# Another place modulo 256 bytes for fourteen w1 products behind each Strassen chunk, and a Strassen chunk directly behind w2

## The chip, the core and the metric

The kernel runs on one core of one Trainium2 chip. The metric is the device time of one execution in microseconds (us), from runs on the chip; before the change it is 2177.1 us, the median of three runs (2176.02 to 2177.48). TensorE (PE in the rows) multiplies, VectorE (DVE) and ScalarE (ACT) prepare operands, SyncE (SP) issues the DMAs.

## What is computed

Two transformer layers over 256 tokens of width 2048: stick-breaking attention and an MLP, then native sparse attention and an MLP, all in float32. The change touches the two MLPs alone.

```python
D_MODEL, SEQ, D_FF = 2048, 256, 4 * 2048

def sqrelu_mlp(h, w1, w2):
    return jnp.square(jax.nn.relu(h @ w1)) @ w2

for layer in range(DEPTH):          # DEPTH = 2
    h = h + attention[layer](rms_norm(h, g_attention[layer]))
    h = h + sqrelu_mlp(rms_norm(h, mlp_norm_g[layer]), mlp_w1[layer], mlp_w2[layer])
```

## The kernel before

Every float32 product is made of three products in a faster 32-bit format: an operand is split into a high part (`hi`, made by ScalarE) and the rest (`lo`, made by VectorE as operand minus `hi`), and `hi*hi + hi*lo + lo*hi` is summed in PSUM. Weights come in **chunks** of 512 KB: `load` issues one DMA from SP's queue into one of five `raw` buffers, `split` makes `hi` and `lo` of it, in one of four buffers each. A buffer of the pool is free again when its last reader is done.

The hidden width of 8192 is done in four groups (`fg` 0 to 3) of 2048. In `mlp`, `group1` multiplies by 2048 columns of w1, in four blocks (`fb` 0 to 3) of 512 columns with eight chunks each; `group2` then multiplies the squared result by the matching 2048 rows of w2. There are three kinds of chunk:

- a **w1 chunk** (`chunk_T`, L186): the weights are the stationary operand (128x128), x is the moving one (256 columns). 24 products: for each of eight 128x128 tiles, `hi` with `xhi` and with `xlo` (16 products), then `lo` with `xhi` (8 products).
- a **w2 chunk** (`chunk_N`, L156): y is stationary, the weights are moving (512 columns); 12 products.
- a **Strassen chunk** (`chunk_S`, L253): a part of w2 (column blocks 2 and 3 of four) that is done with seven instead of eight block products, by sums of weights (`ts`, made by VectorE, then split) and sums of y (`ss`); 21 products with 256 moving columns. Its own split `shi`, `slo` has a single buffer. VectorE makes `ts` in three steps (L226, L232, L233), then `slo` (L234) and the `lo` of the sums (L136). After eight such chunks `add_S` reads their four PSUM banks (pool `att`, four buffers).

`group2` does column blocks 0 and 1 as 16 w2 chunks and lays the eight Strassen chunks of block 2 between them, the i-th after w2 chunk j with j >= 2 + 1.6 i. Block 3 of group `fg` is done as eight Strassen chunks beside w1 of group `fg + 1`: `step`, behind chunks 2 and 5 of each block of w1. Only the last group does block 3 within `group2`, and group 0's w1 has no Strassen chunks beside it. So there are six w1 stages with eight Strassen chunks each, three in each MLP.

`split` puts a tile's data at an offset within its buffer, in elements of four bytes: `NEAR` 0, `TURN` 8, `FAR` 16, `SUM` 48, `SUM0` 60. All these buffers, and x, y and `ss`, begin at 128 modulo 256 bytes, so that `FAR` begins at 192, `TURN` at 160, `SUM` at 64 and `SUM0` at 112 modulo 256. Before the change w1 chunks lie at `FAR`, except the first of a stage with Strassen chunks, which lies at `TURN`; Strassen chunks beside w2 have `shi` at `SUM0`, those beside w1 have it at `SUM`; w2 chunks lie at `NEAR`.

The order of the work on each engine follows the order of the code for TensorE; a scheduler places the VectorE and ScalarE instructions between, so their order is read from the built program.

Of the kernel before, what the change touches and what calls it, by code (L numbers as in the profile page):

```python
# [8 lines left out]
F32 = mybir.dt.float32  # L9
F32R = mybir.dt.float32r  # L10
AF = mybir.ActivationFunctionType
OP = mybir.AluOpType
# [3 lines left out]
P = 128  # L16
# [3 lines left out]
KD = D // P  # L20
NB = 512
# [4 lines left out]
KC = 2  # L26
# [13 lines left out]
def hybrid_kernel(  # L40
# [6 lines left out]
    nc = tc.nc  # L47
# [4 lines left out]
    whi = ctx.enter_context(tc.tile_pool(name="whi", bufs=4))  # L52
    wlo = ctx.enter_context(tc.tile_pool(name="wlo", bufs=4))
# [70 lines left out]

    PAD = 64
    NEAR, FAR, TURN, SUM, SUM0 = 0, 16, 8, 48, 60

# [9 lines left out]
    def load(src, k0, nk, n0, nn):  # L139
        raw = wraw.tile([P, nk, nn], F32, tag="raw", name="raw")  # L140
        nc.sync.dma_start(
            raw, src[k0 * P:(k0 + nk) * P, n0:n0 + nn].rearrange("(k p) n -> p k n", p=P)
        )
        return raw

    def load_split(*where, o=(NEAR, NEAR)):
        return split(load(*where), o)
# [27 lines left out]
                mm(ahi, lo[:, kk, :], k, t, False, last and kk == KC - 1)  # L175
            pump()

    def chunk_T(ps, src, k0, n0, first, last, nk=KC, o=None):

        nm = KC * NB // P // nk  # L180
        hi, lo = src if isinstance(src, tuple) else load_split(src, k0, nk, n0, nm * P, o=o or (FAR, FAR))
        tiles = [(kk, m) for kk in range(nk) for m in range(nm)]

        def mm(w, x, kk, m, s, e):
            o = ps[m // 2][:, (m % 2) * T:(m % 2 + 1) * T]
            nc.tensor.matmul(o, w[:, kk, m * P:(m + 1) * P], x[:, k0 + kk, :], start=s, stop=e, skip_group_check=True)  # L186

        for kk, m in tiles:
            mm(hi, xhi, kk, m, first and kk == 0 and m % 2 == 0, False)
            mm(hi, xlo, kk, m, False, False)  # L190
        pump()
        for kk, m in tiles:
            mm(lo, xhi, kk, m, False, last and kk == nk - 1)
        pump()

    def proj_T(ps, src, n0, nk=KC, turn=False, then={}):

        for i in range(KD // nk):
            k0 = i * nk
            o = TURN if turn and i == 0 else FAR  # L200
            chunk_T(ps, src, k0, n0, k0 == 0, k0 + nk == KD, nk, (o, o))
            if i in then:
                then[i]()

# [192 lines left out]
    def mlp(l, layer, junk, done, last=None):  # L397
        w1, w2 = mlp_w1[l], mlp_w2[l]
        ss = junk.tile([P, 2, KD // 2, 4, P], F32R, name="ss", bufs=1)
        row = junk.tile([P, T], F32, name="row", bufs=1)  # L400

        def rows():
            yield
            pb = bcast_rows(make_rstd(layer))
            nc.scalar.activation(row, pb[:, :T], AF.Copy)

        def in_S(fg, nb, o):

            for i in range(NK):
                if i == 0:  # L410
                    bs, s = banks_S(att, "att")
                chunk_S(s, w2, fg * KD + i * KC, nb * NB, i == 0, i == NK - 1, yhi, ylo, ss[:, 0], ss[:, 1],
                        koff=fg * KD, o=o)
                if i == NK - 1:
                    add_S(nb, bs, s, junk)
                yield

        def group1(fg, beside_w1):

            step = lambda: next(beside_w1)  # L420
            for fb in range(D // NB):
                ps = [bank(acc, "acc") for _ in range(NB // P // 2)]
                proj_T(ps, w1, fg * D + fb * NB, turn=fg > 0 and fb == 0,
                       then={2: step, 5: step} if beside_w1 else {})
                k, n = fb * (NB // P), NB // P
                a = junk.tile([P, n, T], F32, tag="pre", name="pre", bufs=1)
                for j in range(0, n, 2):
                    nc.vector.scalar_tensor_tensor(
                        a[:, j:j + 2, :], ps[j // 2].rearrange("p (m t) -> p m t", m=2), 0.0,
                        row.unsqueeze(1).to_broadcast([P, 2, T]), op0=OP.max, op1=OP.mult,  # L430
                    )
                s = junk.tile([P, n, T], F32, tag="sq", name="sq", bufs=1)
                nc.scalar.activation(s, a, AF.Square)
                nc.scalar.activation(yhi[:, k:k + n, :], s, AF.Copy)
                nc.vector.tensor_tensor(ylo[:, k:k + n, :], s, yhi[:, k:k + n, :].bitcast(F32), op=OP.subtract)

                sv = s.rearrange("p (j kk) t -> p j kk t", kk=2)
                a1, a2 = [[sv[:, :, kk, t * P:(t + 1) * P] for kk in (1, 0)] for t in range(NT)]
                q = junk.tile([P, 2, 4, P], F32, tag="sums", name="sums", bufs=1)
                nc.vector.scalar_tensor_tensor(q[:, :, 0, :], a2[0], -1.0, a2[1], op0=OP.mult, op1=OP.subtract)  # L440
                nc.vector.tensor_tensor(q[:, :, 2, :], a1[0], a2[0], op=OP.subtract)
                nc.vector.tensor_tensor(q[:, :, 1, :], a2[1], q[:, :, 2, :], op=OP.subtract)
                nc.vector.tensor_tensor(q[:, :, 3, :], a1[1], q[:, :, 1, :], op=OP.subtract)
                split_evac(ss[:, 0, k // 2:k // 2 + 2], ss[:, 1, k // 2:k // 2 + 2], q)

        def group2(fg, end):

            blocks = (0, 1, 3) if end else (0, 1)
            side, si = in_S(fg, 2, SUM0), 0
            for j in range(len(blocks) * NK):  # L450
                nb, i = blocks[j // NK], j % NK
                if i == 0:
                    ps = [bank(acc, "acc") for _ in range(NT)]
                out = last is not None and end and nb == 3
                chunk_N(ps, w2, fg * KD + i * KC, nb * NB, i == 0, i == NK - (2 if out else 1), yhi, ylo,
                        koff=fg * KD, by_token=out and i == NK - 1)
                if i == NK - 1:
                    if out:
                        add_out(nb, ps, last)
                        return  # L460
                    add_h(nb, ps)
                    if end and nb == 3:
                        done(nb, (att, "att"))
                if si < NK and j >= (3 + 1.75 * si if end else 2 + 1.6 * si):
                    next(side)
                    si += 1
                    if si == NK and end:
                        for n in range(3):
                            done(n, (att, "att"))

        spawn(rows(), 1)
        NK = KD // KC
        for fg in range(DFF // D):
            group1(fg, in_S(fg - 1, 3, SUM) if fg else None)
            group2(fg, fg == DFF // D - 1)


# [595 lines left out]
```

## Time and profile before

| | |
|---|---|
| median of three runs | 2177.1 us |
| the profiled execution | 2184.2 us, of which 2180.6 us from its first to its last instruction |
| TensorE busy | 2168.8 us (99%) |
| VectorE, ScalarE busy | 1593.0 us, 1188.2 us |
| granted TensorE clock | 0.999 of full speed over the span |
| six w1 stages with Strassen chunks | 109.53 us each |

The table is to be read from the top down: TensorE has hardly any idle time, so a shorter kernel needs fewer or shorter products, and a longer one needs TensorE to wait. Matmuls are pipelined, so a row's length in the timeline (its second number) overlaps the next row; what a piece of work costs is the distance from its start to the start of the next.

### The profile page before, as it was taken

To read this page: it belongs to the slowest core of one execution; us is meant where nothing else is said; L and a number is where in the kernel's file an instruction comes from. 1 tells how busy PE (TensorE), PEld (TensorE's weight loads), DVE (VectorE), ACT (ScalarE), POOL (GpSimd) and SP (SyncE) were. 2 spreads that over 40 slices of the span, in tenths; PEclk is the share of its full clock that TensorE was granted. 3 is DMA by queue.
4 is the path that set the end of the run, shared out by engine and by line. 5 is a ranking of instruction groups with operands and counts; after the bars stand their busy time and mean duration, and the time that the engine had idled before them with its cause. 6 is when DMAs were issued, how large, how long until landed. Compare 5 with 4: busy or idle time off the path is not lost.

```text
span 2180.6 us, 37293 instructions
## 1 busy us (share of the span) xinstructions
PE 2168.8 (99%) x14914; PEld 2000.9 (92%) x14914; DVE 1593.0 (73%) x2190; ACT 1188.2 (54%) x1591; POOL 42.5 (2%) x75
## 2 busy tenths in 40 slices
PE   9999999999999999999999999999999999999999
PEld 9999988998998999999898888889989989999998
DVE  4655556668778878778777877755778788787786
ACT  5555565545555455555546666654554545554553
POOL 0000000000000000000000011000000000000000
PEclk9999999999999999999999999999999999999999
DMA  7655555665665665665667554456556556656664
GB/s 223 204 176 173 164 174 176 187 198 178 209 194 183 203 194 185 221 194 182 201 183 221 164 145 135 137 164 188 181 201 190 191 182 215 198 176 212 194 196 162
DMA packets 260790, 406.35 MB, mean 186 GB/s; under 512 B 13188, under 2 KB 91912, under 8 KB 260616
## 3 DMA queue, kind: packets, MB, share of 16 engines
q1 hardware_dynamic: 259800, 403.52, 59.3%
q8 instruction: 116, 1.90, 0.4%
q10 hardware_dynamic: 816, 0.46, 0.1%
q14 instruction: 58, 0.48, 0.1%
HBM read 401.83 MB, written 2.10 MB: 185 GB/s over the span
## 4 chain that ended last, share of the span: by engine, by line
PE 96%; DVE 2%; DMA 1%; ACT 0%; issue 0%; POOL 0%; DVEq 0%; ACTq 0%; SPq 0%; POOLq 0%
PE acc L186 43%; PE acc L156 35%; PE att L253 12%; PE att L156 1%; DMA raw<-in_mlp_w_dram 1%; DVE lo L136 1%; PE att L310 1%; PE att L905 1%; PE att L897 0%; PE att L898 0%; PE att L899 0%; PE att L592 0%; PE att L640 0%; PE att L851 0%; DVE slo L234 0%
## 5 line engine op out<-in xcount | busy, mean ns | idle before, releaser
L134 ACT ACTIVATE hi<-raw 128x1024 fp32r<-128x1024 f32 x639 | 672.8, 1057 | 503.4 <-PE acc L186 229.0
L136 DVE TENSOR_TENSOR lo<-raw,hi 128x1024 fp32r<-128x1024 f32 x639 | 776.4, 1221 | 224.5 <-ACT hi L134 206.2
L186 PE MATMUL acc<-xs,hi 128*128 128x256 f32 x5360 | 679.5, 280 | 1.9 <-ACT hi L134 1.9
L186 PEld LDWEIGHTS acc<-xs,hi 128*128 128x128 f32 x5360 | 647.8, 189 | 3.1 <-ACT hi L134 2.1
L186 PE MATMUL acc<-xs,lo 128*128 128x256 f32 x2680 | 366.5, 280 | 0.0
L186 PEld LDWEIGHTS acc<-xs,lo 128*128 128x128 f32 x2680 | 335.7, 189 | 0.0
L156 PE MATMUL acc<-hi,yhi 128*128 128x512 f32 x828 | 324.9, 393 | 0.0
L156 PE MATMUL acc<-hi,ylo 128*128 128x512 f32 x828 | 323.3, 391 | 0.0
L134 ACT ACTIVATE hi<-ts 128x1024 fp32r<-128x1024 f32 x112 | 118.4, 1057 | 195.0 <-DVE ts L233 121.8
L156 PE MATMUL acc<-lo,yhi 128*128 128x512 f32 x828 | 223.1, 391 | 0.0
L226 DVE TENSOR_TENSOR ts<-raw 128x512 f32<-128x512 f32 x112 | 77.4, 691 | 169.9 <-DMA raw<-in_mlp_w_dram 169.7
L156 PEld LDWEIGHTS acc<-lo,yhi 128*128 128x128 f32 x828 | 154.6, 188 | 31.9 <-issue 0.4
L156 PEld LDWEIGHTS acc<-hi,ylo 128*128 128x128 f32 x828 | 155.7, 188 | 29.5 <-DVE ylo L297 0.2
L156 PEld LDWEIGHTS acc<-hi,yhi 128*128 128x128 f32 x828 | 155.6, 188 | 29.6 <-ACT yhi L296 0.2
L156 PE MATMUL acc<-hi,xs 128*128 128x512 f32 x704 | 177.2, 392 | 0.0
L156 PEld LDWEIGHTS acc<-hi,xs 128*128 128x128 f32 x704 | 130.4, 188 | 26.5
L136 DVE TENSOR_TENSOR lo<-ts,hi 128x1024 fp32r<-128x1024 f32 x112 | 136.6, 1220 | 12.0 <-ACT hi L134 11.2
L231 ACT ACTIVATE shi<-raw 128x768 fp32r<-128x768 f32 x112 | 94.0, 839 | 65.0 <-DMA raw<-in_mlp_w_dram 38.3
L234 DVE TENSOR_TENSOR slo<-raw,shi 128x768 fp32r<-128x768 f32 x112 | 106.6, 952 | 0.0
L156 PE MATMUL acc<-lo,xs 128*128 128x512 f32 x352 | 97.5, 397 | 0.0
L253 PE MATMUL att<-hi,ss 128*128 128x256 f32 x672 | 94.8, 277 | 0.0
L253 PEld LDWEIGHTS att<-hi,ss 128*128 128x128 f32 x672 | 85.5, 188 | 0.0
(248 smaller groups left out, 2132.2 us busy)
## 6 DMA issues: line engine op xcount, KB each, us to landing
raw<-in_mlp_w_dram SPq DMA_DIRECT2D x512, 512.0 KB, 4.3
raw<-in_sb_w_qkv_dram SPq DMA_DIRECT2D x95, 512.0 KB, 3.8
raw<-in_nsa_w_in_dram SPq DMA_DIRECT2D x50, 512.0 KB, 3.8
raw<-in_sb_w_out_dram SPq DMA_DIRECT2D x32, 512.0 KB, 4.0
raw<-in_nsa_w_in_dram SPq DMA_DIRECT2D x64, 256.0 KB, 3.4
raw<-in_nsa_w_out_dram SPq DMA_DIRECT2D x32, 512.0 KB, 3.7
w1t<-in_nsa_cmp_w_dram SPq DMA_DIRECT2D x8, 512.0 KB, 4.8
h<-in_x_dram SPq DMA_DIRECT2D x8, 256.0 KB, 4.8
```

The lines of the kernel that those rows point to most:

```text
L134: nc.scalar.activation(hi, raw, AF.Copy)
L136: nc.vector.tensor_tensor(lo, raw, hi.bitcast(F32), op=OP.subtract)
L156: mm = lambda a, b, k, t, s, e: nc.tensor.matmul(ps[t], a[:, k, t * P:(t + 1) * P], b, start=s, stop=e)
L186: nc.tensor.matmul(o, w[:, kk, m * P:(m + 1) * P], x[:, k0 + kk, :], start=s, stop=e, skip_group_check=True)
L226: nc.vector.tensor_tensor(ts[:, :2, :], flat[:, W:3 * W].rearrange("p (a n) -> p a n", a=2), b12, op=OP.subtract)
L231: nc.scalar.activation(hi, flat[:, :3 * W], AF.Copy)
L234: nc.vector.tensor_tensor(lo, flat[:, :3 * W], hi.bitcast(F32), op=OP.subtract)
L253: nc.tensor.matmul(ps[i], a, w, start=s, stop=e, skip_group_check=True)
L310: nc.tensor.transpose(ps[:, j * T + t * P:j * T + (t + 1) * P], h[:, t, (kp + j) * P:(kp + j + 1) * P], ident)
L905: nc.tensor.transpose(ptp[:w, j * P:(j + 1) * P], src(j), ident)
```

## The change

It does three things in both MLPs.

1. `group1` does the first Strassen chunk before its first w1 chunk, thus directly behind the last w2 chunk of the group before, with `shi` at `SUM0`; the second comes behind chunk 4 of block 0, the others behind chunks 2 and 5 of blocks 1 to 3 as before.
2. The w1 chunk right behind a Strassen chunk that stands beside w1 (seven in a stage) is split by the new `split_turn`: `hi` lies at `TURN` for seven of its eight tiles (fourteen products) and at `FAR` for the eighth, `lo` at `FAR`. ScalarE and VectorE do the split in two pieces, of 896 and 128 elements, where it was one of 1024. The first w1 chunk of the stage stays wholly at `TURN`; it now has a Strassen chunk ahead of it.
3. In `group2` (all groups but the last) the Strassen chunks come at j >= 1.5 + 1.5 i, so behind w2 chunks 2, 3, 5, 6, 8, 9, 11, 12, where they were behind 2, 4, 6, 7, 9, 10, 12, 14.

```diff
+    def split_turn(raw):
+        flat = raw.rearrange("p k n -> p (k n)")
+        n, c = KC * NB, KC * NB - P
+        h, l = whi.tile([P, n + PAD], F32R, tag="hi", name="hi"), wlo.tile([P, n + PAD], F32R, tag="lo", name="lo")
+        for a, b, o in ((0, c, TURN), (c, n, FAR)):
+            nc.scalar.activation(h[:, o + a:o + b], flat[:, a:b], AF.Copy)
+            nc.vector.tensor_tensor(
+                l[:, FAR + a:FAR + b], flat[:, a:b], h[:, o + a:o + b].bitcast(F32), op=OP.subtract
+            )
+        cut = lambda t, o: [t[:, o(j) + j * P:o(j) + (j + 1) * P] for j in range(n // P)]
+        return cut(h, lambda j: TURN if (j + 1) * P <= c else FAR), cut(l, lambda j: FAR)
...
     def proj_T(ps, src, n0, nk=KC, turn=False, then={}):
         for i in range(KD // nk):
             k0 = i * nk
-            o = TURN if turn and i == 0 else FAR
-            chunk_T(ps, src, k0, n0, k0 == 0, k0 + nk == KD, nk, (o, o))
+            o = (TURN, TURN) if turn and i == 0 else None if i - 1 in then else (FAR, FAR)
+            chunk_T(ps, src, k0, n0, k0 == 0, k0 + nk == KD, nk, o)
...
-                        koff=fg * KD, o=o)
+                        koff=fg * KD, o=o if i == 0 else o1)
...
         def group1(fg, beside_w1):
             step = lambda: next(beside_w1)
+            if beside_w1:
+                step()
             for fb in range(D // NB):
                 proj_T(ps, w1, fg * D + fb * NB, turn=fg > 0 and fb == 0,
-                       then={2: step, 5: step} if beside_w1 else {})
+                       then={i: step for i in ((2, 5) if fb else (4,))} if beside_w1 else {})
...
-                if si < NK and j >= (3 + 1.75 * si if end else 2 + 1.6 * si):
+                if si < NK and j >= (3 + 1.75 * si if end else 1.5 + 1.5 * si):
...
-            group1(fg, in_S(fg - 1, 3, SUM) if fg else None)
+            group1(fg, in_S(fg - 1, 3, SUM0, SUM) if fg else None)
```

(`chunk_T` with `o` None takes the tiles from `split_turn`; its products are the same, in the same order. A w1 stage has the same 32 w1 chunks and eight Strassen chunks before and after.)

**Where TensorE goes from w2 to w1.** In the first stage with Strassen chunks TensorE went from the last w2 chunk (L156, its `hi` and `lo` parts) straight into the first w1 chunk (L186); two more w1 chunks and then a Strassen chunk followed.

```order
L156 MATMUL acc<-hi,yhi 128x512
L156 MATMUL acc<-hi,ylo 128x512
L156 MATMUL acc<-lo,yhi 128x512 x4
L186 MATMUL acc<-xs,hi 128x256 x16
L186 MATMUL acc<-xs,lo 128x256 x8
```

Now the same first w1 chunk (here L206) follows the end of a Strassen chunk (L273), which follows w2; four more w1 chunks come before the next Strassen chunk.

```order
L273 MATMUL att<-hi,yhi 128x256
L273 MATMUL att<-hi,ylo 128x256
L273 MATMUL att<-slo,yhi 128x256 x2
L273 MATMUL att<-slo,ss 128x256
L273 MATMUL att<-lo,ss 128x256 x3
L273 MATMUL att<-lo,yhi 128x256
L206 MATMUL acc<-xs,hi 128x256 x16
L206 MATMUL acc<-xs,lo 128x256 x8
```

What moved is one Strassen chunk, from behind the third w1 chunk to ahead of the first; the turned first chunk now follows products of Strassen's shape and place.

**VectorE between the `slo` of two neighbouring Strassen chunks in w2.** In the first MLP's first `group2`, before: from `slo_5305` (the Strassen chunk behind w2 chunk 9) to `slo_5358` (the one behind chunk 10, with only that w2 chunk between them). `ts_5426` belongs to the next Strassen chunk, the `lo` from a `raw` to w2 chunks.

```order
L234 TENSOR_TENSOR slo_5305<-raw_5300,shi_5304 128x768
L136 TENSOR_TENSOR lo_5339<-raw_5335,hi_5337 128x1024
L232 TENSOR_TENSOR ts_5355<-ts_5355,raw_5353 128x256
L233 TENSOR_TENSOR ts_5355<-raw_5353,ts_5355 128x256
L136 TENSOR_TENSOR lo_5365<-ts_5355,hi_5363 128x1024
L226 TENSOR_TENSOR ts_5426<-raw_5424 128x512
L136 TENSOR_TENSOR lo_5392<-raw_5388,hi_5390 128x1024
L232 TENSOR_TENSOR ts_5426<-ts_5426,raw_5424 128x256
L233 TENSOR_TENSOR ts_5426<-raw_5424,ts_5426 128x256
L234 TENSOR_TENSOR slo_5358<-raw_5353,shi_5357 128x768
```

After, in the same `group2`, the last two Strassen chunks (`slo_5411` behind w2 chunk 11, `slo_5464` behind chunk 12). `ts_5565` belongs to the Strassen chunk that now follows w2 directly; its `raw_5563` takes the `raw` buffer that `lo_5445` frees.

```order
L254 TENSOR_TENSOR slo_5411<-raw_5406,shi_5410 128x768
L137 TENSOR_TENSOR lo_5445<-raw_5441,hi_5443 128x1024
L137 TENSOR_TENSOR lo_5471<-ts_5461,hi_5469 128x1024
L246 TENSOR_TENSOR ts_5565<-raw_5563 128x512
L137 TENSOR_TENSOR lo_5507<-raw_5503,hi_5505 128x1024
L252 TENSOR_TENSOR ts_5565<-ts_5565,raw_5563 128x256
L254 TENSOR_TENSOR slo_5464<-raw_5459,shi_5463 128x768
```

There is less VectorE work between the two `slo` than in the pair of before, but one step in it waits for a DMA that could only be issued two instructions earlier; and there are now four such pairs in a `group2` (behind chunks 2 and 3, 5 and 6, 8 and 9, 11 and 12) where there were two (6 and 7, 9 and 10).

## Rows read from the trace of the kernel before

**Rows 1.** The page: busy time; chain of waits by engine and by line.

```profile
PE 2168.8 (99%) x14914; PEld 2000.9 (92%) x14914; DVE 1593.0 (73%) x2190; ACT 1188.2 (54%) x1591; POOL 42.5 (2%) x75
...
PE 96%; DVE 2%; DMA 1%; ACT 0%; issue 0%; POOL 0%; DVEq 0%; ACTq 0%; SPq 0%; POOLq 0%
PE acc L186 43%; PE acc L156 35%; PE att L253 12%; PE att L156 1%; DMA raw<-in_mlp_w_dram 1%; DVE lo L136 1%; PE att L310 1%; PE att L905 1%; PE att L897 0%; PE att L898 0%; PE att L899 0%; PE att L592 0%; PE att L640 0%; PE att L851 0%; DVE slo L234 0%
```

**Rows 2.** Windows, L186 alone: stretch, length, busy (count), clock, DMA share, GB/s.

```profile
415.69:486.41 70.72, 70.72 (x626) 70.68 (x624) 1.00 0.67 192
550.27:659.80 109.53, 91.54 (x768) 90.75 (x767) 1.00 0.63 197
722.77:832.30 109.53, 91.54 (x768) 90.75 (x767) 1.00 0.62 193
...
1982.24:2091.77 109.53, 91.54 (x768) 90.76 (x767) 1.00 0.62 196
```

**Rows 3.** Timeline, TensorE, one w1 stage: start, length, instructions merged, count.

```profile
722.77 2.06 PE L186 MATMUL acc<-xs,hi 128*128 128x256 f32 x16
724.66 1.11 PE L186 MATMUL acc<-xs,lo 128*128 128x256 f32 x8
725.61 1.98 PE L186 MATMUL acc<-xs,hi 128*128 128x256 f32 x16
...
728.33 1.98 PE L186 MATMUL acc<-xs,hi 128*128 128x256 f32 x16
...
731.05 0.28 PE L253 MATMUL att<-shi,yhi 128*128 128x256 f32 x1
...
733.52 2.05 PE L186 MATMUL acc<-xs,hi 128*128 128x256 f32 x16
...
736.35 2.05 PE L186 MATMUL acc<-xs,hi 128*128 128x256 f32 x16
...
739.18 2.05 PE L186 MATMUL acc<-xs,hi 128*128 128x256 f32 x16
...
742.01 0.29 PE L253 MATMUL att<-shi,yhi 128*128 128x256 f32 x1
...
744.41 2.04 PE L186 MATMUL acc<-xs,hi 128*128 128x256 f32 x16
...
832.30 0.40 PE L156 MATMUL acc<-hi,yhi 128*128 128x512 f32 x1
```

**Rows 4.** Timeline: a Strassen chunk within w2, and what follows it.

```profile
717.61 0.28 PE L253 MATMUL att<-shi,yhi 128*128 128x256 f32 x1
...
720.02 0.39 PE L156 MATMUL acc<-hi,yhi 128*128 128x512 f32 x1
```

**Rows 5.** Waits of TensorE, 500:1010, then 1575:2180: total us, times, longest.

```profile
PE att L253 <- DVE slo L234: 1.0, 2, 0.6
...
PE att L253 <- DVE slo L234: 1.8, 2, 1.1
```

**Rows 6.** Timeline, VectorE, then TensorE, at neighbouring Strassen chunks; idle before in brackets.

```profile
522.12 0.95 DVE L234 TENSOR_TENSOR slo<-raw,shi 128x768 fp32r<-128x768 f32 x1
...
526.19 1.23 DVE L136 TENSOR_TENSOR lo<-ts,hi 128x1024 fp32r<-128x1024 f32 x1 [1.19 <-ACT hi L134]
...
529.87 0.95 DVE L234 TENSOR_TENSOR slo<-raw,shi 128x768 fp32r<-128x768 f32 x1
...
530.87 0.50 PE L253 MATMUL att<-slo,yhi 128*128 128x256 f32 x2 [0.60 <-DVE slo L234]
```

**Rows 7.** The page: groups (count, busy, mean ns, idle before, releaser); DMA issues.

```profile
L136 DVE TENSOR_TENSOR lo<-raw,hi 128x1024 fp32r<-128x1024 f32 x639 | 776.4, 1221 | 224.5 <-ACT hi L134 206.2
...
L226 DVE TENSOR_TENSOR ts<-raw 128x512 f32<-128x512 f32 x112 | 77.4, 691 | 169.9 <-DMA raw<-in_mlp_w_dram 169.7
...
L234 DVE TENSOR_TENSOR slo<-raw,shi 128x768 fp32r<-128x768 f32 x112 | 106.6, 952 | 0.0
...
raw<-in_mlp_w_dram SPq DMA_DIRECT2D x512, 512.0 KB, 4.3
```

More of the change, by code (lines that the diff above doesn't have):

```diff
@@ L176, in chunk_N, with chunk_T @@
             pump()
-    def chunk_T(ps, src, k0, n0, first, last, nk=KC, o=None):
+    def split_turn(raw):
[9 more added lines that the diff above has]
+        return cut(h, lambda j: TURN if (j + 1) * P <= c else FAR), cut(l, lambda j: FAR)
+    def chunk_T(ps, src, k0, n0, first, last, nk=KC, o=(FAR, FAR)):
         nm = KC * NB // P // nk
-        hi, lo = src if isinstance(src, tuple) else load_split(src, k0, nk, n0, nm * P, o=o or (FAR, FAR))
         tiles = [(kk, m) for kk in range(nk) for m in range(nm)]
+        if o is None:
+            hi, lo = split_turn(load(src, k0, nk, n0, nm * P))
+        else:
+            hi, lo = [
+                [w[:, kk, m * P:(m + 1) * P] for kk, m in tiles]
+                for w in (src if isinstance(src, tuple) else load_split(src, k0, nk, n0, nm * P, o=o))
+            ]
         def mm(w, x, kk, m, s, e):
             o = ps[m // 2][:, (m % 2) * T:(m % 2 + 1) * T]
[L186 to L190, printed above, removed]
+            nc.tensor.matmul(o, w, x[:, k0 + kk, :], start=s, stop=e, skip_group_check=True)
+        for (kk, m), w in zip(tiles, hi):
+            mm(w, xhi, kk, m, first and kk == 0 and m % 2 == 0, False)
+            mm(w, xlo, kk, m, False, False)
         pump()
-        for kk, m in tiles:
-            mm(lo, xhi, kk, m, False, last and kk == nk - 1)
+        for (kk, m), w in zip(tiles, lo):
+            mm(w, xhi, kk, m, False, last and kk == nk - 1)
         pump()
@@ L405, in rows, with in_S @@
             nc.scalar.activation(row, pb[:, :T], AF.Copy)
-        def in_S(fg, nb, o):
+        def in_S(fg, nb, o, o1):
             for i in range(NK):
@@ L448, in group2 @@
             blocks = (0, 1, 3) if end else (0, 1)
-            side, si = in_S(fg, 2, SUM0), 0
+            side, si = in_S(fg, 2, SUM0, SUM0), 0
             for j in range(len(blocks) * NK):
```

## Prediction

> **What bounds the kernel now.** I read the page first: TensorE is busy 99% of the span, and the chain of waits runs over TensorE for 96% of it; w1 and the other products of its form (L186) have 43%, w2 (L156) 35%, Strassen (L253) 12% [rows 1]. So a gain has to come from TensorE's own pace, and a loss from a wait that it does not have now. VectorE is at 73% [rows 1].
>
> Then the windows of L186. In the first w1 stage, which has no Strassen chunks, 624 products take 70.72 us, which is 113.3 ns for each; the six stages with Strassen chunks take 109.53 us each (three of the six are shown, the others have the same length), at a granted clock of 1.00 like the first [rows 2]. Such a stage has 768 w1 products and 8 x 21 Strassen products; at 113.3 ns the 936 would take 106.1 us. So 3.4 us of each stage is a slower pace that no clock and no wait explains.
>
> The timeline shows where. The first chunk, turned, takes 2.84 us (722.77 to 725.61), the two behind it 2.72 us each (113.3 ns for a product). The Strassen chunk at 731.05 takes 2.47 us (118 ns), and from there a w1 chunk takes 2.83 us (733.52 to 736.35 to 739.18; 117.8 ns) [rows 3]. The instructions, shapes, offsets and clock of the chunk at 725.61 and the one at 736.35 are the same. So there are **two paces for the same product**, and TensorE stays in one until a product of another kind comes: a turned chunk led into the fast one, the Strassen chunk into the slow one. The next Strassen chunk, entered from the slow pace, takes 2.40 us (742.01 to 744.41) and yet slow w1 follows [rows 3]. The stage ends at 832.30 with w2.
>
> **The fourteen turned products.** They remove nothing; their effect is on the chunks behind them. If they lead into the fast pace, as the turned chunk at 722.77 did, a stage is (where nothing else stands, from [rows 3]):
> - the Strassen chunk directly behind w2, like the ones within w2: 717.61 to 720.02, 2.41 us [rows 4]
> - the turned first chunk: 2.84 us
> - 24 chunks at the fast pace: 24 x 2.72 = 65.28 us
> - 7 Strassen chunks entered from the fast pace: 7 x 2.47 = 17.29 us
> - 7 chunks with fourteen turned products. The turned `hi` part has 16 products in 1.89 us (722.77 to 724.66), 118.1 ns each: 14 x 118.1 + 10 x 113.3 = 2.79 us, and 2.84 if all 24 go at the turned pace. I take 2.79, since the first unturned product behind the turned chunk is already fast: 7 x 2.79 = 19.53 us.
>
> Together 107.35 us against 109.53, 2.18 us less; six stages: **13.1 us**. Bounds: if no turned chunk works, 24 x 2.72 becomes 4 x 2.72 + 20 x 2.83 (the first chunk, still wholly turned, serves four), one Strassen chunk takes 2.47 and six 2.40, and the seven chunks 2.83: 109.4, a gain of 0.7 us in all. If the wholly turned first chunk fails too, now that a Strassen chunk stands ahead of it, 2.41 + 2.84 + 24 x 2.83 + 7 x (2.40 + 2.83) = 109.8, a loss of 1.5 us. No row shows fourteen turned products, or a turned chunk behind a Strassen chunk: the six turned chunks in the trace all stand behind w2 and all have 24. That is the main doubt, since the exit from a turned chunk may depend on how many products it has.
>
> **The split in two pieces.** On VectorE 1024 elements take 1221 ns and 768 take 952 [rows 7]: 1.05 ns an element and some 145 ns fixed, so a second piece costs 145 ns; ScalarE, at 54% [rows 1], gets a second piece as well. 42 chunks have it, 6 us of VectorE in all, none of it on the path: the w1 stages show no wait of TensorE at all in the lists of waits, which hold only L253 for `slo` (L234) [rows 5], and those fall in w2. Without that cover it would cost at most 6 us. The faster w1 asks VectorE for the same work in 2% less time, and it is 73% busy.
>
> **The moved Strassen chunks in w2.** Now two Strassen chunks stand with one w2 chunk between them at four places of a `group2` instead of two. `slo` has one buffer, so the second `slo` cannot be made before the first is used. The trace shows what that costs: VectorE made the first `slo` at 522.12, waited 1.19 us for ScalarE on the way, came to the second at 529.87, and TensorE stood 0.60 us until 530.87 [rows 6]: 7.75 us between the two `slo` were too many. All such waits together are 2.8 us, the longest 1.1 [rows 5]. In the new order the worst pair is the last. Between its two `slo` stand `slo`, a `lo`, a `lo`, the first `ts` step, a `lo` and a short `ts` step, by the steps between starts about 0.9 + 1.1 + 1.1 + 0.6 + 1.1 + 0.5 = 5.3 us, which would be no stall. But the `ts` step needs a buffer that the first of those `lo` frees; a DMA takes 4.3 us to land, and VectorE already waits for DMAs at this step 170 us in 112 cases, 1.5 us each [rows 7]. With 1.1 us of other work in between the wait is up to 3.2 us, so 5.3 to 8.5 us between the `slo`. Where 7.75 gave 0.6 us, 8.5 gives 1.35, and 5.3 gives none. I take 0.7 at that pair in each of the six `group2` that change, 4.0 us, in place of the 2.8 now: **1.2 us lost**; from 2.8 gained (no pair waits) to what the last rival says.
>
> **The Strassen chunk behind w2** reads PSUM banks that `add_S` must have left. Three w2 chunks, about 8.2 us, lie between the end of the chunk before and it, and its first product on such a bank comes some 0.8 us later. From the `slo` of the chunk before, wanted 0.8 us before that chunk's end, to `add_S`'s last read of these banks VectorE has three `lo` (1.2 us each), one `slo` (0.95) and six short steps (0.3 to 0.7, as the ones above): about 7.5 us [rows 7] in 9.8. I cost it at nothing; if that cover were gone, the wait would be a microsecond or two in six places.
>
> **Sum.** 13.1 gained, 1.2 lost, 11.9 us less. The profiled execution took 2184.2 us, so I expect 2172.3 in its terms, 0.5%; the median of the runs lies 7.1 below it, and 2177.1 - 11.9 = **2165.2 us**.
>
> **A rule that speaks against it.** The two paces above show the same instructions at 113.3 and 117.8 ns [rows 2, 3]. The Trainium skill's page "SBUF — State Buffer", section "Who interferes with whom", gives TensorE two independent read ports, one for the moving operand and one for the weights, and lets only the port pair that VectorE shares with GpSimd cause contention. By that rule the place of an operand cannot set the pace, and the turning would be worth nothing. The rows show a difference that follows neither clock nor shape, so I hold the rule as incomplete here; the rival just below carries its chance.
>
> **Rivals.**
> 1. *The turning does nothing behind a Strassen chunk.* For it: nothing in the trace shows it there, and a Strassen chunk entered from either pace left the slow one behind it [rows 3]. Against it: a turned chunk led into the fast pace from w2 each of six times. Time: 2177.1 - 0.7 + 1.2 = 2177.6, and with the first chunk failing too 2177.1 + 1.5 + 1.2 = 2179.8. By the page's rule on the ports it would also be about that.
> 2. *It works every other time*: it fails behind a Strassen chunk entered fast (2.47 us) and works behind one entered slow (2.40 us). Then the chunks behind turns one, three, five and seven (5, 4, 4 and 1) stay slow and ten chunks of 24 are fast: 2.41 + 2.84 + 10 x 2.72 + 14 x 2.83 + 4 x (2.47 + 2.83) + 3 x (2.40 + 2.79) = 108.8; six times 0.7, less 1.2: 2174.1.
> 3. *Slower: VectorE comes too late for the second `slo`.* Place: the pairs behind w2 chunks 5 and 6, 8 and 9, 11 and 12, eighteen places. If each cost 1.3 us, somewhat over the longest now, that is 23.4 less the 2.8 there now: 2177.1 - 13.1 + 20.6 = 2184.6. It decides from 15.9 / 18 = 0.9 us at each. For it: VectorE's waits for DMAs; against: the 5.3 us of work, and that only four waits are listed for the twelve such pairs of now [rows 5].
>
> **How the numbers follow.** Forecast 0.60 (2162 to 2169); rival 1 0.24, of which 0.16 at 2177.6 and 0.08 at 2179.8; rival 2 0.07; rival 3 0.09. The lower end takes the forecast with no wait left in w2, 2177.1 - 13.1 - 2.8 = 2161.2. Up to 2178.5 lie the forecast, rival 2 and the larger part of rival 1, 0.83. A measurement can tell about 0.2% (4.4 us): faster has the forecast and a little of rival 2, 0.62; slower rival 3 and a little of rival 1, 0.10; the rest, 0.28, is the same.
>
> **What would show it.** In the new trace: w1 stages of about 107.4 us; w1 chunks of 2.72 us from the second chunk behind each Strassen chunk on (2.83: rival 1; by turns: rival 2); Strassen chunks beside w1 of 2.47; waits of TensorE for L234's successor of about 4 us in all (over 16: rival 3). The forecast is wrong above all if the fourteen products end where the pace falls back.

## The result, and the profile after

The changed kernel takes 2192.1 us (median of 8 runs, 2182.4 to 2194.5); the kernel before takes 2178.5 beside it (8 runs). The ratio is 1.0055, 95% interval 1.0039 to 1.0072: **slower by about 12 us** (13.5 by the medians), where 12 us less was forecast. Two executions of the runs below, at granted clocks of 0.85 and 0.76 over their whole span, are left out of every figure. The profiled execution took 2194.2 us, of which 2192.5 are its span.

On the page after (its lines on busy time and on the chain of waits by engine, and one of its groups: busy, mean ns, idle before, releaser) the chain that set the end leaves TensorE far more often than in [rows 1]:

```profile
PE 2160.9 (99%) x14914; PEld 1989.1 (91%) x14914; DVE 1590.7 (73%) x2232; ACT 1188.8 (54%) x1633; POOL 42.5 (2%) x75
...
PE 80%; DVE 10%; DMA 6%; issue 3%; ACT 1%; POOL 0%; DVEq 0%; ACTq 0%; SPq 0%; POOLq 0%
...
L246 DVE TENSOR_TENSOR ts<-raw 128x512 f32<-128x512 f32 x112 | 77.4, 691 | 198.7 <-DMA raw<-in_mlp_w_dram 198.4
```

TensorE is on 80% of the chain (96% before), DMAs on 6% (1%). VectorE is no busier, but stands 198 us for DMAs at the first `ts` step, 170 before [rows 7].

The w1 stages did what was forecast. Windows of w1's line (L206 now; length, busy, clock, DMA share, GB/s), then TensorE's timeline of one stage (start, length, merged count):

```profile
725.14:832.56 107.42, 88.80 (x768) 88.31 (x768) 1.00 0.60 192
903.34:1010.76 107.42, 88.81 (x768) 88.31 (x768) 1.00 0.62 197
```

```profile
727.56 2.05 PE L206 MATMUL acc<-xs,hi 128*128 128x256 f32 x16
...
730.40 2.00 PE L206 MATMUL acc<-xs,hi 128*128 128x256 f32 x16
...
741.30 0.28 PE L273 MATMUL att<-shi,yhi 128*128 128x256 f32 x1
...
743.78 2.04 PE L206 MATMUL acc<-xs,hi 128*128 128x256 f32 x16
```

All six are 107.42 us (109.53 in [rows 2], 107.35 forecast). The wholly turned chunk takes 2.84 (727.56 to 730.40), four fast ones 10.90, the Strassen chunk 2.48; behind each Strassen chunk the fast pace comes back. That is 12.7 us less.

w2 lost more than that. From the start of w2 to the next stage the six took 382.3 us in all before and 405.4 after, **23.1 us more**; the rest of the span is 1.5 longer. Two of the six w2 stand behind the first w1 of an MLP, which has no Strassen chunks; they lost 2.4 us together, and the four behind stages with Strassen chunks lost 20.7. Windows of TensorE over the third w2 of the first MLP, of the kernel before and of the changed one (length, busy, clock, DMA share, GB/s):

```profile
832.30:895.92 63.62, 63.26 (x362) 1.00 0.60 198
```

```profile
832.56:903.34 70.78, 65.15 (x363) 0.98 0.57 186
```

TensorE's waits over the whole trace (total us, times, longest), and the two longest in that w2 in its timeline, with the idle time in brackets:

```profile
PE att L273 <- DVE slo L254: 14.2, 17, 2.4
PE att L273 <- ACT shi L251: 7.7, 4, 3.2
```

```profile
849.26 0.57 PE L273 MATMUL att<-shi,yhi 128*128 128x256 f32 x1 [3.20 <-ACT shi L251]
...
853.38 0.40 PE L157 MATMUL acc<-hi,yhi 128*128 128x512 f32 x1
...
894.23 0.50 PE L273 MATMUL att<-slo,yhi 128*128 128x256 f32 x2 [2.43 <-DVE slo L254]
```

Before, the waits for `slo` were 2.7 us, and none for `shi` was listed. The four waits for `shi` come one in each of the four w2 behind stages with Strassen chunks, at its second Strassen chunk, and are its first wait. So the waits do not fall on the last pair alone, which I had priced.

**Where the loss is made.** I worked out a *lead* from the trace: how long the `lo` of the first w2 chunk was ready before its first product. VectorE's `lo` for the first chunk of the w2 just shown, and TensorE's first products with it:

```profile
831.81 1.22 DVE L137 TENSOR_TENSOR lo<-raw,hi 128x1024 fp32r<-128x1024 f32 x1
```

```profile
834.40 1.07 PE L157 MATMUL acc<-lo,yhi 128*128 128x512 f32 x4
```

831.81 + 1.22 = 833.03, so 1.4 us. At the same w2 of the kernel before, 827.68 + 1.22 to 834.14 is 5.2 us:

```profile
827.68 1.22 DVE L136 TENSOR_TENSOR lo<-raw,hi 128x1024 fp32r<-128x1024 f32 x1
```

```profile
834.14 1.07 PE L156 MATMUL acc<-lo,yhi 128*128 128x512 f32 x4
```

At the three other w2 behind a stage with Strassen chunks the lead was 3.2, 2.5 and 3.6 us (before 7.0, 4.0 and 6.8). TensorE did not wait in w1, but VectorE fell behind there, and w2 started with less in hand. The experiments ask why.

### The profile page after: what moved, and what is told of

Its sections match the earlier page's. It is cut to its first block, busy times and chain, and to the rows that moved or that the text cites. A ratio compares the mean times of both kernels' runs of the same rounds, so it can differ in the third digit from the quotient of the medians.

```text
span 2192.5 us, 37357 instructions
## 1 busy us (share of the span) xinstructions
PE 2160.9 (99%) x14914; PEld 1989.1 (91%) x14914; DVE 1590.7 (73%) x2232; ACT 1188.8 (54%) x1633; POOL 42.5 (2%) x75
## 4 chain that ended last, share of the span: by engine, by line
PE 80%; DVE 10%; DMA 6%; issue 3%; ACT 1%; POOL 0%; DVEq 0%; ACTq 0%; SPq 0%; POOLq 0%
PE acc L206 40%; PE acc L157 27%; PE att L273 7%; DMA raw<-in_mlp_w_dram 6%; DVE lo L137 4%; DVE slo L254 2%; PE att L157 1%; DVE ts L246 1%; PE att L330 1%; DVE ts L252 1%; PE att L927 1%; PE att L919 0%; ACT hi L135 0%; DVE ylo L457 0%; DVE pre L450 0%
## 5 line engine op out<-in xcount | busy, mean ns | idle before, releaser
L137 DVE TENSOR_TENSOR lo<-raw,hi 128x1024 fp32r<-128x1024 f32 x597 | 725.0, 1220 | 225.8 <-ACT hi L135 208.6
L135 ACT ACTIVATE hi<-raw 128x1024 fp32r<-128x1024 f32 x597 | 627.8, 1057 | 439.3 <-PE acc L157 176.6
L206 PE MATMUL acc<-xs,hi 128*128 128x256 f32 x5360 | 669.8, 278 | 1.9 <-ACT hi L135 1.9
L206 PEld LDWEIGHTS acc<-xs,hi 128*128 128x128 f32 x5360 | 638.9, 188 | 2.6 <-ACT hi L135 2.1
L206 PE MATMUL acc<-xs,lo 128*128 128x256 f32 x2680 | 360.5, 277 | 0.0
L206 PEld LDWEIGHTS acc<-xs,lo 128*128 128x128 f32 x2680 | 330.4, 188 | 0.0
L273 PE MATMUL att<-hi,ss 128*128 128x256 f32 x672 | 96.4, 280 | 0.0
L273 PEld LDWEIGHTS att<-hi,ss 128*128 128x128 f32 x672 | 87.0, 190 | 0.0
```

Of the source, the lines that this page charges most:

```text
L135: nc.scalar.activation(hi, raw, AF.Copy)
L137: nc.vector.tensor_tensor(lo, raw, hi.bitcast(F32), op=OP.subtract)
L206: nc.tensor.matmul(o, w, x[:, k0 + kk, :], start=s, stop=e, skip_group_check=True)
L273: nc.tensor.matmul(ps[i], a, w, start=s, stop=e, skip_group_check=True)
```

## The experiments

Diffs are against the changed kernel. One edit comes back often; **"no chunk behind w2"** stands for:

```diff
             if beside_w1:
-                step()
...
-                       then={i: step for i in ((2, 5) if fb else (4,))} if beside_w1 else {})
+                       then={i: step for i in (2, 5)} if beside_w1 else {})
...
-            group1(fg, in_S(fg - 1, 3, SUM0, SUM) if fg else None)
+            group1(fg, in_S(fg - 1, 3, SUM, SUM) if fg else None)
```

"Stages" and "w2" are the sums in us over the six w1 stages with Strassen chunks and over the six w2 that lead into them, worked out from each run's trace; "lead" is that at the w2 just shown (the third of the first MLP). Ratios are to the kernel before on the same chip. A trace is one execution, and executions of one kernel lie up to 18.5 us apart here (e1_turn), so a ratio need not follow its trace exactly: the trace of e5_turn_pace is 8 us slower than the median of its runs, those of e9_one_lo, e6_raw6 and e4_old_pace are their quickest, that of e14_after_at5 its slowest. Where trace and ratio differ, the ratio decides.

| run | stages | w2 | lead | ratio (95%) |
|---|---|---|---|---|
| before | 657.2 | 382.3 | 5.2 | 1 |
| after | 644.5 | 405.4 | 1.4 | 1.0055 (1.0039 to 1.0072) |
| e1_turn | 645.2 | 390.5 | 1.7 | 1.0017 (1.0001 to 1.0033) |
| e2_pace | 657.2 | 379.2 | 6.7 | 0.9993 (0.9984 to 1.0002) |
| e3_no_turn | 656.1 | 393.1 | 3.6 | 1.0070 (1.0057 to 1.0082) |
| e4_old_pace | 661.6 | 389.5 | 2.1 | 1.0115 (1.0097 to 1.0132) |
| e5_turn_pace | 645.2 | 388.9 | 3.5 | 0.9977 (0.9961 to 0.9993) |
| e6_raw6 | 644.5 | 396.2 | 4.1 | 1.0031 (1.0017 to 1.0046) |
| e7_hi16 | 650.3 | 380.8 | 6.3 | 0.9970 (0.9958 to 0.9981) |
| e8_pace_raw6 | 657.2 | 386.6 | 6.6 | 1.0047 (1.0031 to 1.0063) |
| e9_one_lo | 645.2 | 381.5 | 5.2 | 0.9969 (0.9958 to 0.9980) |
| e10_pieces | 657.2 | 378.7 | 7.1 | 0.9994 (0.9986 to 1.0003) |
| e11_after_one_lo | 644.5 | 402.5 | 2.0 | 1.0049 (1.0030 to 1.0067) |
| e12_all24 | 651.4 | 383.2 | 5.4 | 0.9972 (0.9962 to 0.9982) |
| e13_second_at5 | 655.5 | 382.5 | 6.7 | 1.0008 (0.9999 to 1.0017) |
| **e14_after_at5** | 644.5 | 388.7 | 5.5 | **0.9968 (0.9957 to 0.9980)** |
| e15_one_lo_at5 | 644.5 | 387.5 | 6.4 | 0.9977 (0.9967 to 0.9986) |

### One part at a time

e1_turn: no chunk behind w2, and the old places in w2.

```diff
-                if si < NK and j >= (3 + 1.75 * si if end else 1.5 + 1.5 * si):
+                if si < NK and j >= (3 + 1.75 * si if end else 2 + 1.6 * si):
```

> Only the fourteen turned products; the order of the Strassen chunks is the one of the kernel before in w1 and in w2. Three theories on the 23 us that w2 of the changed kernel lost. Order: four Strassen pairs instead of two in a group2 ask VectorE for `slo` too soon; then w2 here is as before (about 63.7 us a group2), the w1 stage 2.84 + 23 x 2.72 + 8 x 2.79 + 8 x 2.47 = 107.5 us instead of 109.5, and the time 12 us below the kernel before. Lead: the faster w1 brings TensorE to w2 with VectorE further behind; then w2 here is longer by 12 us or more and the time no better than before. Split: the extra pieces on VectorE and ScalarE delay what w2 needs; then as for lead.

e2_pace: no chunk behind w2, and no turned products.

```diff
-            o = (TURN, TURN) if turn and i == 0 else None if i - 1 in then else (FAR, FAR)
+            o = (TURN, TURN) if turn and i == 0 else (FAR, FAR)
```

> Only the closer places of the Strassen chunks in w2 (due at 1.5 + 1.5 x si instead of 2 + 1.6 x si); no turned products, no Strassen chunk behind w2. Order: w1 stage 109.5 us, the six group2 longer by 15 to 23 us in all, TensorE's waits for `slo` and `shi` of about 20 us, time 15 to 23 us above the kernel before. Lead or split: w2 within 5 us of before, time within 5 us.

e3_no_turn has this last diff alone, and e4_old_pace the diff of e1_turn alone.

> The changed kernel without the fourteen turned products; the order in w1 and w2 is the changed one. Order: w1 stage 109.4 us, w2 longer by the same 23 us in all, time 23 us above the kernel before. Lead or split: w2 within 5 us of before, since w1 is as slow as before and nothing is split in two; time within 5 us.

> The changed kernel with the places of the Strassen chunks in w2 as before (2 + 1.6 x si). The last Strassen chunk of w2 then stands one w2 chunk ahead of the one directly behind w2, which uses the same PSUM banks. Order: the twelve places within w2 as before (about 3 us of waits), but at the end of each of the six w2 a wait for `add_S` of 3 to 4 us, some 20 us in all, w1 stages without it 107.5: time 5 to 12 us above the kernel before. If `add_S` is early enough: 12 us below the kernel before, and the closer places were not needed.

My first theory, that the closer places ask VectorE for `slo` too soon, fell. With the closer places alone TensorE's waits for `slo` nearly vanish; in the whole trace of e2_pace they are

```profile
PE att L273 <- DVE slo L254: 0.6, 2, 0.4
```

so four pairs instead of two cost nothing; w2 is 3.1 us shorter than before. Instead each of the other two edits lengthens w2, although neither changes w2's own products: turned products by 9.7 us (e5_turn_pace, below, against e2_pace), the chunk behind w2 by 13.9 (e3_no_turn against e2_pace), both by 26.2. None of the three theories had said this: e3_no_turn came out neither at the 23 us nor within the 5 that its expectation gave, and in e1_turn w2 is 8.2 us longer than before, where its expectation had none, or 12 and more. e4_old_pace, with waits for `slo`, also shows what the closer places are for. Its list of waits has the `add_S` step (L300) that they avoid:

```profile
PE att L273 <- DVE uv L300: 7.6, 6, 1.6
```

Its stages are 17.1 us longer than the changed kernel's, more than these waits: in three of the six, w1 was slow for the whole stage (the last section). Its time, 25 us above the kernel before, missed the 5 to 12 that were expected.

### Is it the ring of `raw`, the pieces, or the pace?

e5_turn_pace: no chunk behind w2. e6_raw6:

```diff
-    wraw = ctx.enter_context(tc.tile_pool(name="wraw", bufs=5))
+    wraw = ctx.enter_context(tc.tile_pool(name="wraw", bufs=6))
...
-                pT = at.tile([P, 2, NB], F32R, tag="pT", name="pT", bufs=3)
+                pT = at.tile([P, 2, NB], F32R, tag="pT", name="pT", bufs=2)
```

e8_pace_raw6: e2_pace with the diff of e6_raw6. e7_hi16: no chunk behind w2, and sixteen turned products in one piece:

```diff
-            o = (TURN, TURN) if turn and i == 0 else None if i - 1 in then else (FAR, FAR)
+            o = (TURN, TURN) if turn and i == 0 else (TURN, FAR) if i - 1 in then else (FAR, FAR)
```

> The changed kernel without the Strassen chunk directly behind w2: turned products and the closer places in w2 are kept. New theory (supply): VectorE and its ring of five `raw` buffers can just feed the slow w1; it stands 17.4 us for DMAs in a w1 stage of the kernel before, 8.8 with the closer places alone, 22.6 to 23.3 where w1 is fast, so the lead of the weights at the start of w2 shrinks from 5.2 us (6.7 with the closer places alone) to 1.7 and w2 waits. Then here the stage is 107.5 us, and the lead at w2 between 1.7 and 5, so w2 keeps some waits, fewer than with the old places: time 3 to 9 us below the kernel before. Rival (each edit by itself): the Strassen chunk behind w2 causes the loss; then w2 is as with the closer places alone (63.1 us), time 12.7 + 3.3 = 16 us below.

> The changed kernel with six `raw` buffers instead of five (the 4 KB come from the attention's third buffer of `pT`, used outside the MLPs alone). Supply: a sixth DMA can be on its way while VectorE works, its waits at the `ts` step fall from 198 us below 130, the lead at w2 is 5 us or more, TensorE's waits for `slo` and `shi` fall from 21.9 to under 4 us, each w2 to about 63 us: time 13 to 18 us below the kernel before, plus what the attention loses. Rival (the one `slo` buffer): the second `slo` of a pair waits for the first one's last product whatever the DMAs do; then the waits stay at 15 us or more and the time above the kernel before.

> As the run without the Strassen chunk behind w2, but behind each Strassen chunk all sixteen products of `hi` are turned, so that nothing is split in two pieces. Fourteen matters: the chunks behind stay at 2.83 us and the stage at 109.4. Only the turn matters: 16 x 118.1 + 8 x 113.3 = 2.80 us for such a chunk, stage 2.84 + 23 x 2.72 + 8 x 2.80 + 8 x 2.47 = 107.6 us. Supply: 48 pieces less on VectorE, 145 ns each, 7 us in all, give back up to 1.2 us of lead in each stage: time 0 to 4 us below the run with fourteen.

> The closer places alone, with six `raw` buffers and two of `pT`: what the buffers cost or give where w1 is slow and TensorE hardly waits. Supply: within 2 us of the closer places alone (which stand at 0.9993 of the kernel before), as there is no wait left to remove; VectorE's waits at the `ts` step fall below 100 us. If the attention needs the third `pT`, the time is some us longer, all of it in the NSA stretch.

e5_turn_pace came out as expected. The sixth buffer did not: e8_pace_raw6 is slower than e2_pace, with nothing else changed in the MLPs. VectorE's timeline at the end of a w1 block shows why:

```profile
748.62 1.23 DVE L137 TENSOR_TENSOR lo<-raw,hi 128x1024 fp32r<-128x1024 f32 x1 [1.27 <-ACT hi L135]
752.36 0.69 DVE L246 TENSOR_TENSOR ts<-raw 128x512 f32<-128x512 f32 x1 [2.51 <-DMA raw<-in_mlp_w_dram]
...
753.89 1.28 DVE L448 SCALAR_TENSOR_TENSOR pre<-acc,row 128x512 f32<-128x512 f32 x2
```

The scheduler has put the three `ts` steps of a later Strassen chunk ahead of `pre` (the step that reads w1's finished sums out of PSUM), here and at the end of blocks 0 to 2 of each stage with Strassen chunks, and VectorE, in order, stands 2.51 us for the DMA with `pre` queued behind. So this pair does not test the size of the ring, since it changed the order too, and the question is left open. Nor is it the lead that shrank here (6.6 us): why its w2 is 7.4 us longer than e2_pace's no run shows. But it gave the next theory.

The pieces were tested by three more, and 24 turned products by a fourth. e9_one_lo: no chunk behind w2, and one `lo`; e11_after_one_lo: one `lo` alone. e10_pieces: e5_turn_pace with both pieces at `FAR`. e12_all24: as e7_hi16 with `(TURN, TURN)`. The diffs of `split_turn` for one `lo`, then for e10_pieces (the tile's size and the places that `cut` returns change to match):

```diff
-        for a, b, o in ((0, c, TURN), (c, n, FAR)):
...
+        nc.scalar.activation(h[:, TURN:TURN + n], flat, AF.Copy)
+        nc.scalar.activation(h[:, FAR + n:FAR + n + P], flat[:, c:n], AF.Copy)
+        nc.vector.tensor_tensor(l[:, FAR:FAR + n], flat, h[:, TURN:TURN + n].bitcast(F32), op=OP.subtract)
...
```

```diff
-        for a, b, o in ((0, c, TURN), (c, n, FAR)):
+        for a, b, o in ((0, c, FAR), (c, n, FAR)):
...
```

> The run without the Strassen chunk behind w2, with the same fourteen turned products at the same places, but `lo` made by one instruction of VectorE: ScalarE writes all of `hi` at the turned place and its last 128 columns a second time at the other. Theory (pieces): the second piece of `lo`, which stood behind other work on VectorE, held `raw` back and the DMA of a later Strassen chunk's `raw` with it; then the stage is 107.53 us as with two pieces, the w2 about 63.2 instead of 65.5, the waits at the `ts` step fall from 177 us to 145 or less, and the time is 12 us below the closer places alone, some 13 below the kernel before. Rival (pace): w1 itself is too fast for VectorE; then w2 stays at 65 us or more and the time at 0.997 to 0.998 of the kernel before.

> The closer places alone, with the chunks behind Strassen chunks split in two pieces on ScalarE and VectorE, but both at the old place: nothing is turned, so w1 keeps its slow pace (stage 109.53). Pieces: the lead of the weights at w2, 6.7 us without them, falls to some 4 us, the waits at the `ts` step rise from 128 us to about 165, and w2 loses up to 1 us each: 0 to 6 us above the closer places alone. Pace: no change of lead or time, within 1 us.

> The changed kernel with `lo` of the turned chunks made by one instruction, as above. What the Strassen chunk behind w2 costs by itself: without turned products it cost 13.9 us in the six w2 and gave 1.1 in the stages. If the two costs add: stage 107.42, w2 12 to 14 us longer in all than with the closer places alone, time about 0 to 3 us above the kernel before, 8 to 12 below the changed kernel. If the pieces were the cause of all of it: w2 63.2, time 13 us below the kernel before.

> The run without the Strassen chunk behind w2, with all 24 products behind each Strassen chunk turned, in one piece. Sixteen turned products left the chunks behind fast after a Strassen chunk entered slow, and slow after one entered fast; fourteen left them fast each time. If the number decides and 24 behaves as behind w2: all chunks 2.72, stage 9 x 2.84 + 23 x 2.72 + 7 x 2.47 or thereabouts, 107.9 us, w2 63 to 64, time 9 to 12 us below the kernel before. If 24 behaves as 16: stage 108.4 to 108.8, time 5 to 8 below.

Two pieces cost nothing where w1 is slow (e10_pieces). Where it is fast, one `lo` took 7.4 us off w2 in the trace (e9_one_lo against e5_turn_pace), but this sets the quickest execution of the one beside a slow one of the other, and the two ratios overlap: 13 us below the kernel before were expected of e9_one_lo, 7 came. So no cost of the pieces is clear of noise. e11_after_one_lo keeps nearly all of the loss (its time is 11 us above the kernel before, 0 to 3 were expected): the larger part comes with the chunk behind w2.

### The order on VectorE

VectorE's timeline of the changed kernel at the end of block 0 of a w1 stage:

```profile
749.67 1.22 DVE L137 TENSOR_TENSOR lo<-raw,hi 128x1024 fp32r<-128x1024 f32 x1 [0.63 <-ACT hi L135]
754.87 0.69 DVE L246 TENSOR_TENSOR ts<-raw 128x512 f32<-128x512 f32 x1 [3.97 <-DMA raw<-in_mlp_w_dram]
755.48 1.28 DVE L450 SCALAR_TENSOR_TENSOR pre<-acc,row 128x512 f32<-128x512 f32 x2
756.68 1.21 DVE L137 TENSOR_TENSOR lo<-ts,hi 128x1024 fp32r<-128x1024 f32 x1
```

It is the pattern of e8_pace_raw6, once in each of the six stages: `ts` ahead of `pre`, 3.97 us for a DMA here (2.5 to 4.6 in the six), with `pre` and a `lo` behind. In the built program of before, and in those without a chunk behind w2 (with five `raw` buffers), `pre` and that `lo` come first. With the second Strassen chunk behind w1 chunk 5 instead of 4 they do again. e14_after_at5 is the changed kernel with one number changed; e13_second_at5 has no turned products besides, e15_one_lo_at5 one `lo`.

```diff
-                       then={i: step for i in ((2, 5) if fb else (4,))} if beside_w1 else {})
+                       then={i: step for i in ((2, 5) if fb else (5,))} if beside_w1 else {})
```

> The Strassen chunk behind w2 and the closer places, no turned products, as in the run without them (w2 393.1 us in all, time 1.007 of the kernel before); but the second Strassen chunk of each stage stands behind w1 chunk 5 instead of 4. In the old place the recorded order of VectorE had the first `ts` step of the next Strassen chunk ahead of `pre`, and VectorE stood there 4.6 us for its DMA with `pre` and a `lo` queued behind; with place 5 `pre` comes first, as in the kernel before. Theory (order on VectorE): that wait shrinks to 1 to 2 us, the lead at w2 rises from 3.6 to 6 us or more, the six w2 take 379 to 383 us and the time is within 4 us of the kernel before. Rival (two Strassen chunks near each other at the end of w2 empty the ring of `raw`): w2 stays at 390 us or more, time at 1.005 or more.

> The changed kernel with one number changed: the second Strassen chunk of each stage behind w1 chunk 5 instead of 4, so that on VectorE `pre` stands ahead of the `ts` step again. Turned products, their two pieces and the chunk behind w2 stay. Order on VectorE: w2 falls from 405.4 us to about 389, what the turned products with two pieces cost by themselves, stages 107.42; time about 3 to 6 us below the kernel before, 14 to 18 below the changed kernel. Rival: w2 stays above 400 us.

> The same with `lo` of the turned chunks by one instruction of VectorE: both costs taken away, the chunk behind w2 kept. Stages 107.42, w2 380 to 384 us in all, time 8 to 13 us below the kernel before, as without the chunk behind w2 or a little less. If the chunk behind w2 has a cost of its own that neither the order nor the pieces make, w2 is 390 us or more.

The same place in e14_after_at5:

```profile
742.87 1.22 DVE L137 TENSOR_TENSOR lo<-raw,hi 128x1024 fp32r<-128x1024 f32 x1 [0.94 <-ACT hi L135]
745.17 1.29 DVE L450 SCALAR_TENSOR_TENSOR pre<-acc,row 128x512 f32<-128x512 f32 x2 [1.08 <-PE acc L206]
746.37 1.22 DVE L137 TENSOR_TENSOR lo<-ts,hi 128x1024 fp32r<-128x1024 f32 x1
747.58 0.69 DVE L246 TENSOR_TENSOR ts<-raw 128x512 f32<-128x512 f32 x1
```

The DMA lands behind `pre` and `lo`, and `ts` waits for nothing. What that does to the whole stage shows in VectorE's waits there (total, times, longest), of the changed kernel (725.14 to 832.56) and of this one (718.33 to 825.75):

```profile
DVE ts L246 <- DMA raw<-in_mlp_w_dram: 23.3, 8, 4.7
```

```profile
DVE ts L246 <- DMA raw<-in_mlp_w_dram: 7.7, 6, 2.6
DVE pre L450 <- PE acc L206: 3.2, 3, 1.1
```

23.3 us become 7.7, and VectorE now waits for TensorE at `pre`: it is ahead again. The lead at the next w2 is 820.87 + 1.22 to 827.59, 5.5 us (1.4):

```profile
820.87 1.22 DVE L137 TENSOR_TENSOR lo<-raw,hi 128x1024 fp32r<-128x1024 f32 x1
```

```profile
827.59 1.07 PE L157 MATMUL acc<-lo,yhi 128*128 128x512 f32 x4
```

At the three other w2 behind such stages it is 7.1, 6.9 and 6.4. w2 falls by 16.7 us (405.4 to 388.7) and the ratio from 1.0055 to 0.9968, at equal stages. Without turned products the same number takes it from 1.0070 to 1.0008. The rival, that two Strassen chunks near each other at the end of w2 empty the ring, expected w2 above 400 us and is out for most of the loss.

Two things stay open. The number moves a Strassen chunk as well as the order on VectorE, and no run changes the order with the place kept; for the order speak the waits at `ts` just shown. And the order does not always cost: in e3_no_turn it is the same in all six stages, but 12.8 of the 13.9 us fall in the first MLP, while in the second, at waits of 2.4 to 3.4 us, VectorE is ahead again by the end of the stage (leads of 6.3 and 7.6 us at the two w2 there). So it seems to cost only where VectorE does not catch up before w2.

e15_one_lo_at5 missed its expectation: w2 387.5, not 380 to 384. Whether the chunk behind w2 keeps a cost of its own when `pre` comes first is not shown: w2 is 6.0 us longer than without it there (against e9_one_lo), 3.3 in e13_second_at5 (against e2_pace) and 0.2 shorter in e14_after_at5 (against e5_turn_pace), and in each of these pairs the ratios overlap.

So e14_after_at5, e9_one_lo, e7_hi16 and e12_all24 all beat the kernel before by 0.3% (6 to 7 us) and cannot be told apart. In the first two the stages are 12.7 and 12.0 us shorter, and about half of that is given back elsewhere; in the last two the stages are only 6.9 and 5.8 shorter, and nearly all of it stays.

## Why the prediction was wrong

- **The bound and the two paces: right.** w1 behaved as the rows of [rows 2, 3] said, and w2 was where a loss could come from.
- **Turned products: right in size, for a narrower reason than I gave.** 107.42 us for 107.35; 12.7 gained for 13.1. I let fourteen lead into the fast pace like the turned chunk behind w2; e4_old_pace shows that they only keep the pace that TensorE had (the last section). The doubt about their number was the right one: sixteen would have followed the second rival.
- **Two pieces at nothing: not contradicted.** e10_pieces shows no cost at the old pace, and beside a fast w1 none is clear of noise. "None of it on the path", argued from there being no wait of TensorE in w1, was the wrong test: a w1 stage without waits can still hand w2 a smaller lead.
- **The moved Strassen chunks in w2, 1.2 us lost: the sum that missed.** The same waits became 21.9 us instead of 4.0. Its own mechanism was not the cause: by themselves the closer places gained 3.1 in w2 (e2_pace), about the bound of 2.8 gained.
- **The Strassen chunk behind w2 at nothing: the step that failed.** I followed it through `slo`, `add_S` and the PSUM banks, and indeed `add_S` made TensorE wait only with the old places. But I read VectorE's order only in w2. At the end of block 0 in w1 the built program had moved `ts` ahead of `pre`, and the profile's `ts` waits [rows 7] were a warning that I used only for the pair in w2. Price in w2: 13.9 us by itself (e3_no_turn against e2_pace), 16.5 with the turned products (405.4 against 388.9); in time about 17 us in both (ratios 1.0070 against 0.9993, 1.0055 against 0.9977). With `pre` first again (e14_after_at5) the loss is gone.
- **The rivals.** The third had the lists of waits and about the price (20.6 us more waiting in w2, 23.1 measured) but not the cause, which lies a stage earlier, nor quite the place: 7.7 of the 21.9 us of waits are for `shi`, at the second Strassen chunk of a w2. I gave it 0.09, from the 5.3 us of work in a pair, without asking how far ahead VectorE would arrive.
- **One rule.** The Trainium skill's page "SBUF — State Buffer", section "Who interferes with whom", would have made the turning worth nothing. The stages at 107.42 us with the same products contradict it as a full account.

## What to carry to other kernels

Where an engine that prepares operands works ahead, measure how far ahead it is (end of the write to first read) at the border of two stages, before and after; no wait in a stage is no proof that nothing was lost there. When code that a scheduler interleaves is moved, read the built order on every engine at each place where its order differs, not only where the moved work stands, and look for a DMA-fed instruction that has slipped ahead of independent work. Here moving the inserted chunk by one place was worth 19 us (1.0055 to 0.9968), more than the 12.7 that the edit gained in its stages.

## What the runs showed of the hardware

**Fourteen turned products keep the pace; sixteen and 24 swap it.** That is a description of these runs. With fourteen the fast pace came back behind each Strassen chunk of the changed kernel. With sixteen it did so every other time, as my second rival had it for fourteen. TensorE's timeline of e7_hi16:

```profile
734.53 2.05 PE L206 MATMUL acc<-xs,hi 128*128 128x256 f32 x16
...
737.36 2.05 PE L206 MATMUL acc<-xs,hi 128*128 128x256 f32 x16
...
740.19 0.28 PE L273 MATMUL att<-shi,yhi 128*128 128x256 f32 x1
...
742.59 2.05 PE L206 MATMUL acc<-xs,hi 128*128 128x256 f32 x16
...
745.40 1.98 PE L206 MATMUL acc<-xs,hi 128*128 128x256 f32 x16
...
748.12 1.98 PE L206 MATMUL acc<-xs,hi 128*128 128x256 f32 x16
```

The chunk at 734.53 stands behind sixteen turned products that follow a Strassen chunk entered fast, and takes 2.83 us; the next Strassen chunk, entered slow, takes 2.40 (740.19 to 742.59), and behind its sixteen, from 745.40 on, w1 is fast (2.72 to 748.12). 24 alternate in the same way: stages of 108.38 us with sixteen, 108.57 with 24. Nor do fourteen make a slow w1 fast. In e4_old_pace, where TensorE had waited 1.63 us for `add_S` within the Strassen chunk behind w2:

```profile
909.12 2.05 PE L206 MATMUL acc<-xs,hi 128*128 128x256 f32 x16
...
911.94 2.05 PE L206 MATMUL acc<-xs,hi 128*128 128x256 f32 x16
...
920.42 0.29 PE L273 MATMUL att<-shi,yhi 128*128 128x256 f32 x1
...
922.83 2.06 PE L206 MATMUL acc<-xs,hi 128*128 128x256 f32 x16
...
925.66 2.05 PE L206 MATMUL acc<-xs,hi 128*128 128x256 f32 x16
...
928.49 2.05 PE L206 MATMUL acc<-xs,hi 128*128 128x256 f32 x16
```

The 24 turned products behind that chunk led into the slow pace (909.12 to 911.94 is 2.82 us), and behind the fourteen it is still slow (925.66 to 928.49, 2.83) to the end of the stage, 111.83 us. Two more of its stages are like it, behind waits of 1.18 and 1.07 us; in the other three, behind waits of 1.52, 1.00 and 1.23, w1 was fast, so the length of the wait does not decide. No run shows why the number of turned products counts, nor what does decide behind such a wait.

**A wait can cost more than its length.** Windows of TensorE behind three waits of the changed kernel (length, busy, clock, DMA share, GB/s):

```profile
849.26:852.00 2.74, 2.74 (x13) 0.51 0.00 0
...
1768.23:1771.00 2.77, 2.77 (x22) 1.00 0.00 1
894.23:897.00 2.77, 2.77 (x16) 1.00 0.92 297
```

Behind the wait of 3.20 us at 849.26 the granted clock was 0.51, the level of 1.2 GHz, and the Strassen chunk took 4.1 us (849.26 to 853.38) instead of 2.4; behind the waits of 2.08 (1768.23) and 2.43 (894.23) it stayed at 1.00. So that one wait cost 4.9 us.
